# RWKV channel-major projections: inputs prepared ahead of the side work in every step, inverse of heads 0 to 7 from the 21st of 48 steps

## The chip, the cores and the metric

One core of a Trainium2 chip runs the whole forward pass as one program. The metric is the device time of one execution in microseconds; lower is better. The engines that matter here are PE (TensorE, matmuls; its weight loads are listed as PEld), DVE (VectorE), ACT (ScalarE), POOL (GpSimd) and SP, whose queue issues the loads of weights.

## The reference

A two-layer decoder trunk over 512 tokens of width 1024: layer 0 mixes tokens by RWKV-7, layer 1 by a gated MLP, and each layer also has two half-step SwiGLU networks and a cross-attention to 256 memory tokens. The change is in the RWKV-7 mixer, cut here to what matters:

```python
xr, xk, xv = (h + dx * mu[m] for m in (0, 2, 3))       # dx = token_shift(h) - h
r, k, v = xr @ Wr, xk @ Wk, xv @ Wv                    # 512x1024 @ 1024x1024 each
decay = exp(-exp(-softplus(-(w0 + tanh(xw @ w1) @ w2)) - 0.5))
a = sigmoid(a0 + (xa @ a1) @ a2)
kk = (k * k_k), each head of 64 divided by its norm
k = k * (1 + (a - 1) * k_a);  b = kk * a
for each token t, for each of 16 heads:                # state is 64x64
    sa = state @ -kk_t
    state = state * decay_t + sa b_t^T + v_t k_t^T
    y_t = state @ r_t
```

Everything is in fp32.

## The kernel before

**Numbers.** A product in fp32 is made of three matmuls on a rounded high part and a low part of both operands (`mm3`, L114 to L116). The function `split` makes the two parts: ACT casts the high part (L93) and DVE subtracts it for the low part (L98). Weights come in through `wload`: a DMA on SP's queue, then `split` into the tiles `whi` and `wlo`.

**The projection stage** is the function `rwkv_in`, in the profile from about 410 to 615 us. It makes k, r and v (in this order) with channels on the partitions for k and r. The work is cut into 48 steps: 3 projections, for each two column halves `nb`, for each 8 slices of the contraction. One step is `products(i)`: 4 tiles of 3 matmuls, 12 matmuls of 128x512 in all. The first two tiles' low-part products need `wlo` only at the third matmul, L116 for k and r.

**What a step prepares.** `prepare(i + 3)` fetches the weights of the step three ahead: one DMA of 256 KB, one ACT cast (`whi`), one DVE subtraction (`wlo`). In the first half of each projection it also mixes the token-shifted input: an ACT operation (L835), a DVE operation (L837) and a split (ACT L861, DVE L862). The pools hold three weight pairs.

**Side work.** Two kinds of generators are advanced a piece at a time by the same loop. `pump()` advances `post_k` (L994 to L1037: decay, normalisation and gates of the k half just finished) and `post_r` (L1048 to L1073: the same for r), which are mostly DVE and ACT operations on 128x512 or 64x512 tiles with a few matmuls (L975, L1028, L1029, L1072). `invert()` advances `inverse(0)` for heads 0 to 7, once `post_k(0)` is done, and after it `inverse(1)` for heads 8 to 15, once `post_k(1)` is done. The scan over chunks needs the inverses of 64x64 triangular matrices, and `inverse` builds them: scores on PE (L1156, L1163, small matmuls) with copies to `MD` (DVE L1171) and `LT` (ACT L1173), a transposition (DVE L1176), then 30 rounds of forward substitution on DVE, a multiplication and an addition each (L1186, L1193) on 31 to 256 columns, two transpositions (DVE L1203 to `A2`, L1206 to `XT`), copies, and 8 groups of small matmuls (L1225). `inverse(1)` may advance only 8 times in the loop (`ahead`); what is left of it is advanced by the scan's own `pump()` and is finished at the latest before the 9th of 16 chunks.

**Order.** Each engine executes its instructions in the order of the program. That order is made when the program is built, by a scheduler that starts from the order in which the code is written. After the 48 steps a loop finishes `inverse(0)`, and the scan begins: per chunk PE makes `sm` (L1447), DVE (L1452) and ACT copy it to `e`, PE multiplies by the inverse `TT` (L1463), DVE copies to `AV` (L1465), and so on; matmuls of the next work stand between them.

Of the kernel before, what the change touches and what calls it, by code (L numbers as in the profile page):

```python
# [20 lines left out]
KC = C // P  # L21
# [18 lines left out]
class Trunk:  # L40
# [763 lines left out]
    def rwkv_in(self, st, prologue):  # L804
# [28 lines left out]
        def xmix(m, ct):  # L833
            t1 = tp.tile([P, T], F32, tag="xm1", name="xm1")
            act(t1, hT[:, ct, 0:T], AF.Identity, scale=col(MU + m, ct))  # L835
            xm = tp.tile([P, T], F32, tag="xm2", name="xm2")
            nc.vector.scalar_tensor_tensor(  # L837
                xm, hT[:, ct, 1 : T + 1], omu[:, m, ct : ct + 1], t1, ALU.mult, ALU.add
            )
            return xm  # L840
# [10 lines left out]
        def prepare(i):  # L851
            if i >= len(steps):
                return
            p, nb, k = steps[i]
            m, wi = projs[p]
            src = ins["rwkv_w_rkv"][wi, nb, k // 2][:, (k % 2) * 512 : (k % 2) * 512 + 512]
            ws[i] = self.wload(src, 512)
            if nb == 0:
                xm = xmix(m, k)
                xh = xsp.tile([P, 2, T], F32R, tag="xs", name="xs")  # L860
                nc.scalar.copy(xh[:, 0], xm)  # L861
                nc.vector.tensor_tensor(xh[:, 1], xm, xh[:, 0].bitcast(F32), ALU.subtract)  # L862
                xs[p, k] = xh[:, 0], xh[:, 1]
# [72 lines left out]
        def lora_2(ct):  # L936

            cs = slice(ct * P, ct * P + P)
            for j, w in enumerate(w2s):
                ps = sc()  # L940
                self.mm3(ps, [z[:, cs] for z in w], tws, True, True)
                if j == 0:
                    s = tmp("sq")[:, :T]
                    act(s, ps, AF.Sigmoid, bias=col(W0, ct))
                    nc.vector.tensor_tensor_scan(L[:, ct, :], scm, s, 0.0, ALU.mult, ALU.add)
                else:
                    act(AR[ct][:, :, 64:128], c3(ps), AF.Sigmoid, bias=col(A0, ct))
# [4 lines left out]
        def pump():  # L952
            while queue:
                if next(queue[0], 1) is None:
                    break
                queue.pop(0)

        def invert():
            if inv[0] is not None:
                if ready[0] and next(inv[0], 1) is not None:  # L960
                    inv[0] = None
            elif inv[1] is not None and ready[1] and (ahead or self.ttp):
                ahead[:1] = []
                if next(inv[1], 1) is not None:
                    inv[1] = None
# [135 lines left out]
        def products(i, fs=range(4)):  # L1101
            p, nb, k = steps[i]
            x, w = xs[p, k], ws[i]
            for f in fs:
                s = slice(f * P, (f + 1) * P)
                if p == 2:
                    self.mm3(ps[f], [z[:, s] for z in x], w, k == 0, k == KC - 1)
                else:
                    self.mm3(ps[f], [z[:, s] for z in w], x, k == 0, k == KC - 1)
# [9 lines left out]
        for i in range(2, len(steps)):  # L1119
            p, nb, k = steps[i]  # L1120
            if k == 0:
                ps = [self.psum() for _ in range(4)]
            products(i)
            if i < KC:
                lora_2(i)
            else:
                pump()
                invert()
            prepare(i + 3)
            pump()  # L1130
            invert()
            if i == KC - 1:
                act(self.D, L.rearrange("p k (c t) -> p k c t", c=NCH)[:, :, :, CH - 1], AF.Exp, scale=-DECAY)
            if k == KC - 1:
                for f in range(4):
                    evacs[p](nb, f, ps[f])
# [593 lines left out]
```

## Time and profile before

| | us |
|---|---|
| median of 3 runs | 2412.9 (2410.41 to 2415.75) |
| the profiled execution, its own time | 2409.73 |
| span of the profiled execution | 2408.0 |
| PE busy | 2359.3 (98%) |
| DVE busy | 1677.4 (70%) |
| ACT busy | 1087.9 (45%) |
| POOL busy | 136.4 (6%) |

The span is what the engines' records cover; 1.7 us lie around it. Busy shares are of the whole span, in which the projection stage is one part in twelve. The granted clock is TensorE's, as a share of its full 2.4 GHz; over the whole run it was 0.995.

### The profile page before, as it was taken

To read this page: it belongs to the slowest core of one execution; us is meant where nothing else is said; L and a number is where in the kernel's file an instruction comes from. 1 tells how busy PE (TensorE), PEld (TensorE's weight loads), DVE (VectorE), ACT (ScalarE), POOL (GpSimd) and SP (SyncE) were. 2 spreads that over 40 slices of the span, in tenths; PEclk is the share of its full clock that TensorE was granted. 3 is DMA by queue.
4 is the path that set the end of the run, shared out by engine and by line. 5 is a ranking of instruction groups with operands and counts; after the bars stand their busy time and mean duration, and the time that the engine had idled before them with its cause. 6 is when DMAs were issued, how large, how long until landed. Compare 5 with 4: busy or idle time off the path is not lost.

```text
span 2408.0 us, 40219 instructions
## 1 busy us (share of the span) xinstructions
PE 2359.3 (98%) x16336; PEld 2067.2 (86%) x16336; DVE 1677.4 (70%) x2680; ACT 1087.9 (45%) x1821; POOL 136.4 (6%) x157
## 2 busy tenths in 40 slices
PE   7999999989999999999999999999999999999998
PEld 7898995757887888999998999998888888989897
DVE  7776867798877656877777787764254455969594
ACT  5443433975555344534344443443432244535252
POOL 2000001000345000000000000000000000000000
PEclk9999999999999999999999999999999999999999
DMA  4433222213444422324242323242223242233222
GB/s 144 151 100 119 88 99 71 72 46 92 121 98 110 159 88 84 117 75 133 71 132 75 113 89 119 80 153 97 88 88 96 70 132 75 84 97 122 84 97 84
DMA packets 104937, 241.65 MB, mean 100 GB/s; under 512 B 27184, under 2 KB 31280, under 8 KB 104368
## 3 DMA queue, kind: packets, MB, share of 16 engines
q1 hardware_dynamic: 98864, 225.67, 29.6%
q10 hardware_dynamic: 5888, 13.42, 1.7%
q8 instruction: 128, 2.10, 0.4%
q14 instruction: 57, 0.47, 0.1%
HBM read 227.38 MB, written 7.34 MB: 97 GB/s over the span
## 4 chain that ended last, share of the span: by engine, by line
PE 89%; DVE 5%; ACT 3%; DMA 1%; issue 1%; POOL 1%; DVEq 0%; SPq 0%; POOLq 0%; ACTq 0%
PE ps L114 27%; PE ps L116 27%; PE ps L115 27%; PE ps L217 1%; DVE wlo L98 1%; PE y L1514 1%; PE y L1515 1%; PE ps L756 1%; PE sc L1285 0%; ACT whi L93 0%; POOL wlo L96 0%; DMA m_scr<-mo 0%; PE ps L911 0%; PE sm L1479 0%; ACT BK L983 0%
## 5 line engine op out<-in xcount | busy, mean ns | idle before, releaser
L98 DVE TENSOR_TENSOR wlo<-wraw,whi 128x1024 fp32r<-128x1024 f32 (+1 forms) x264 | 281.3, 1069 | 292.5 <-ACT whi L93 277.9
L114 PE MATMUL ps<-nT_hi,whi 128*128 128x256 f32 (+1 forms) x1504 | 449.7, 301 | 4.1 <-ACT nT_hi L93 1.5
L116 PE MATMUL ps<-nT_hi,wlo 128*128 128x256 f32 (+1 forms) x1504 | 448.6, 299 | 1.2 <-POOL wlo L96 1.2
L115 PE MATMUL ps<-nT_lo,whi 128*128 128x256 f32 (+1 forms) x1504 | 449.1, 299 | 0.4 <-DVE nT_lo L98 0.3
L93 ACT CAST whi<-wraw 128x1024 fp32r<-128x1024 f32 (+1 forms) x268 | 246.0, 921 | 355.1 <-PE ps L116 227.4
L114 PEld LDWEIGHTS ps<-nT_hi,whi 128*128 128x128 f32 x1504 | 283.2, 189 | 15.6 <-ACT nT_hi L93 3.3
L115 PEld LDWEIGHTS ps<-nT_lo,whi 128*128 128x128 f32 x1504 | 284.5, 189 | 10.9 <-DVE nT_lo L98 1.5
L116 PEld LDWEIGHTS ps<-nT_hi,wlo 128*128 128x128 f32 x1504 | 284.1, 189 | 11.3 <-POOL wlo L96 1.5
L116 PE MATMUL ps<-whi,hT_lo 128*128 128x512 f32 x704 | 278.5, 396 | 0.0
L114 PE MATMUL ps<-whi,hT_hi 128*128 128x512 f32 x704 | 277.9, 395 | 0.0
L115 PE MATMUL ps<-wlo,hT_hi 128*128 128x512 f32 x704 | 277.7, 394 | 0.0
L116 PE MATMUL ps<-s_hi,wlo 128*128 128x256 f32 x960 | 271.2, 283 | 1.2 <-DVE wlo L98 1.1
L114 PE MATMUL ps<-s_hi,whi 128*128 128x256 f32 x960 | 271.0, 282 | 1.2 <-ACT whi L93 0.6
L115 PE MATMUL ps<-s_lo,whi 128*128 128x256 f32 x960 | 270.4, 282 | 0.0
L93 ACT CAST whi<-g_raw 128x1024 fp32r<-128x1024 f32 x160 | 168.1, 1050 | 200.4 <-PE ps L116 125.6
L98 DVE TENSOR_TENSOR wlo<-g_raw,whi 128x1024 fp32r<-128x1024 f32 x160 | 196.5, 1228 | 32.6 <-ACT whi L93 31.9
L116 PEld LDWEIGHTS ps<-s_hi,wlo 128*128 128x128 f32 x960 | 181.7, 189 | 2.0 <-DVE wlo L98 2.0
L114 PEld LDWEIGHTS ps<-s_hi,whi 128*128 128x128 f32 x960 | 181.6, 189 | 1.6 <-ACT whi L93 0.8
L115 PEld LDWEIGHTS ps<-s_lo,whi 128*128 128x128 f32 x960 | 181.4, 189 | 0.0
L115 PEld LDWEIGHTS ps<-wlo,hT_hi 128*128 128x128 f32 x704 | 132.6, 188 | 31.0
L116 PEld LDWEIGHTS ps<-whi,hT_lo 128*128 128x128 f32 x704 | 132.5, 188 | 30.8
L114 PEld LDWEIGHTS ps<-whi,hT_hi 128*128 128x128 f32 x704 | 132.6, 188 | 30.3
(360 smaller groups left out, 4612.2 us busy)
## 6 DMA issues: line engine op xcount, KB each, us to landing
wraw<-in_ffn_w_out_dram SPq DMA_DIRECT2D x88, 512.0 KB, 4.1
g_raw<-in_ffn_w_in_dram SPq DMA_DIRECT2D x80, 512.0 KB, 3.6
t_raw<-in_ffn_w_in_dram SPq DMA_DIRECT2D x80, 256.0 KB, 3.0
e_raw<-in_ffn_w_in_dram SPq DMA_DIRECT2D x80, 256.0 KB, 3.4
wraw<-in_rwkv_w_rkv_dram SPq DMA_DIRECT2D x48, 256.0 KB, 2.7
wraw<-in_ffn_w_in_dram SPq DMA_DIRECT2D x16, 512.0 KB, 3.6
wraw<-in_xattn_wq_dram SPq DMA_DIRECT2D x16, 512.0 KB, 3.8
wraw<-in_xattn_wo_dram SPq DMA_DIRECT2D x16, 512.0 KB, 3.6
```

What stands on the lines that cost most here:

```text
L93: r = [self.nc.scalar.copy(hi, src)]
L98: r.append(self.nc.vector.tensor_tensor(lo, src, hi.bitcast(F32), ALU.subtract))
L114: mm(ps, l[0], r[0], start=start, stop=False, **kw)
L115: mm(ps, l[0], r[1], start=False, stop=False, **kw)
L116: mm(ps, l[1], r[0], start=False, stop=stop, **kw)
L217: nc.tensor.transpose(ps[:, j * P : (j + 1) * P], xn[:, k * P : (k + 1) * P], self.ident)
L756: nc.tensor.matmul(pv[:, t * P : (t + 1) * P], v[:, t, g * P : (g + 1) * P], ws[:, g, :], start=True, stop=True,)
L1514: mm(o, rz[n % 2][:, par, i, :], SV[:, par, i, :], start=True, stop=False)
L1515: mm(o, M[:, par, i, 64:128], AV[:, par, i, :], start=False, stop=True)
```

## The change

In steps 8 to 47 `prepare(i + 3)` now stands ahead of both calls of `pump()` and `invert()`; before, one of each came first. And `invert()` is called only from step 20 on (the 21st). Steps 0 to 7 keep their order (there is nothing to invert in them). No instruction is added or removed; lines behind L1131 have numbers smaller by one after the change.

```diff
@@ -1123,12 +1123,11 @@
             products(i)
             if i < KC:
                 lora_2(i)
-            else:
+            prepare(i + 3)
+            for _ in range(2 if i >= KC else 1):
                 pump()
-                invert()
-            prepare(i + 3)
-            pump()
-            invert()
+                if i >= 20:
+                    invert()
             if i == KC - 1:
                 act(self.D, L.rearrange("p k (c t) -> p k c t", c=NCH)[:, :, :, CH - 1], AF.Exp, scale=-DECAY)
             if k == KC - 1:
```

What the scheduler makes of it is shown at three places. A row is a line of the code, an operation, and output<-inputs with their buffers' numbers; the numbers of buffers differ between the two kernels.

**DVE, ahead of the low part that came last.** Before, 43 rows stand between the low parts of the weights of step 27 and of step 28 (`wlo_5332`). The last of them are these; `X` and `tmp` are the substitution of `inverse(0)`, `sq` and `AR0` are `post_r(0)`:

```order
L1186 TENSOR_TENSOR tmp_5208<-M2_4973,X_4975 128x252
L1037 TENSOR_TENSOR AR1_3886<-AR1_3886,fe_5223 128x8x64
L1193 TENSOR_TENSOR X_4975<-X_4975,tmp_5208 128x14x18
L1050 TENSOR_TENSOR AR0_3885<-AR0_3885,em_5280 128x8x64
L1186 TENSOR_TENSOR tmp_5229<-M2_4973,X_4975 128x247
L1054 SCALAR_TENSOR_TENSOR sq_5283<-AR0_3885,cols_64,BK0_3893 64x512
L1193 TENSOR_TENSOR X_4975<-X_4975,tmp_5229 128x13x19
L1054 SCALAR_TENSOR_TENSOR sq_5283<-AR0_3885,cols_64,BK0_3893 64x512
L1186 TENSOR_TENSOR tmp_5244<-M2_4973,X_4975 128x240
L1050 TENSOR_TENSOR AR0_3885<-AR0_3885,em_5316 128x8x64
L1193 TENSOR_TENSOR X_4975<-X_4975,tmp_5244 128x12x20
L98 TENSOR_TENSOR wlo_5332<-wraw_5329,whi_5331 128x512
```

Now the low parts of steps 28 and 29 stand 7 and 10 rows behind those ahead of them, and the longest gap is the next one, 25 rows between the low parts of steps 29 and 30 (`wlo_5342`). It ends so:

```order
L1054 SCALAR_TENSOR_TENSOR sq_5286<-AR0_3885,cols_64,BK0_3893 64x512
L1185 TENSOR_TENSOR tmp_5190<-M2_5160,X_5162 128x156
L1054 SCALAR_TENSOR_TENSOR sq_5286<-AR0_3885,cols_64,BK0_3893 64x512
L1192 TENSOR_TENSOR X_5162<-X_5162,tmp_5190 128x26x6
L1050 TENSOR_TENSOR AR0_3885<-AR0_3885,em_5314 128x8x64
L1185 TENSOR_TENSOR tmp_5211<-M2_5160,X_5162 128x175
L1054 SCALAR_TENSOR_TENSOR sq_5317<-AR0_3885,cols_64,BK0_3893 64x512
L1192 TENSOR_TENSOR X_5162<-X_5162,tmp_5211 128x25x7
L1054 SCALAR_TENSOR_TENSOR sq_5317<-AR0_3885,cols_64,BK0_3893 64x512
L1185 TENSOR_TENSOR tmp_5214<-M2_5160,X_5162 128x192
L98 TENSOR_TENSOR wlo_5342<-wraw_5339,whi_5341 128x512
```

The gap is shorter by 18 rows and two steps later, and the substitution in it is at an earlier, narrower round (its last blocks have 175 and 192 elements a partition, where they had 247 and 240).

**DVE, at the start of the scan.** Before, the substitution of `inverse(1)` is over and its transpositions (L1203, L1206) stand just ahead of the first copy `e1` of the scan (L1452):

```order
L1193 TENSOR_TENSOR X_5898<-X_5898,tmp_6884 128x31
L1203 STREAM_TRANSPOSE A2_6917<-X_5898 128x32x32
L98 TENSOR_TENSOR wlo_6353<-wraw_6350,whi_6352 128x512
L1206 STREAM_TRANSPOSE XT_6954<-X_5898 128x32x32
L1452 COPY e1_6319<-sm_6314 128x128
```

Now 17 rounds of the substitution, 34 rows, are spread behind that copy, and the transpositions stand in the fifth chunk, between its `e1` and its copies to `AV`:

```order
L1451 COPY e1_6968<-sm_6963 128x128
L1185 TENSOR_TENSOR tmp_6884<-M2_6029,X_6031 128x31
L1287 TENSOR_TENSOR M_6962<-sc_6977,con_63 128x512
L1192 TENSOR_TENSOR X_6031<-X_6031,tmp_6884 128x31
L1287 TENSOR_TENSOR M_6962<-sc_6978,con_63 128x512
L1202 STREAM_TRANSPOSE A2_6917<-X_6031 128x32x32
L1205 STREAM_TRANSPOSE XT_6954<-X_6031 128x32x32
L98 TENSOR_TENSOR wlo_6999<-wraw_6996,whi_6998 128x512
L1343 TENSOR_TENSOR BK0_3893<-y_6431,g2_6952 128x4x128
L1464 COPY AV_6792<-sm_7017 64x128
L1464 COPY AV_6792<-sm_7024 64x128
```

So the first copy of the scan has lost the two transpositions ahead of it, and the fifth chunk has them.

**PE, at step 18.** Before, the first scores of `inverse(0)` follow the products of step 18:

```order
L114 MATMUL ps_4827<-xs_4706,whi_4698 128x512
L115 MATMUL ps_4827<-xs_4706,whi_4698 128x512
L975 MATMUL pn_4840<-sq_4841,con_63 128x512
L116 MATMUL ps_4827<-xs_4706,wlo_4699 128x512
L1156 MATMUL sc_4735<-AR0_3885,BK0_3893 32x64
L1163 MATMUL sc_4735<-AR0_3885,BK0_3893 32x32
```

Now the products of the next step follow at that place, and the scores stand at steps 21 (64 of them) and 26 (2 times 32) of what were 4 groups of 64:

```order
L115 MATMUL ps_4753<-xs_4694,whi_4686 128x512
L975 MATMUL pn_4779<-sq_4780,con_63 128x512
L116 MATMUL ps_4753<-xs_4694,wlo_4687 128x512
L975 MATMUL pn_4779<-sq_4791,con_63 128x512
L114 MATMUL ps_4750<-xs_4743,whi_4735 128x512
L115 MATMUL ps_4750<-xs_4743,whi_4735 128x512
L116 MATMUL ps_4750<-xs_4743,wlo_4736 128x512
```

The matmuls are the same ones, and the small ones come later.

## Rows read from the trace of the kernel before

**Rows 1.** The page: busy time by engine, and the chain that ended last.

```profile
PE 2359.3 (98%) x16336; PEld 2067.2 (86%) x16336; DVE 1677.4 (70%) x2680; ACT 1087.9 (45%) x1821; POOL 136.4 (6%) x157
...
PE 89%; DVE 5%; ACT 3%; DMA 1%; issue 1%; POOL 1%; DVEq 0%; SPq 0%; POOLq 0%; ACTq 0%
```

**Rows 2.** Busy time in stretches of the stage and of the scan.

```profile
core 0: us, PE busy (x) PEld busy (x) DVE busy (x) ACT busy (x) POOL busy (x), PEclk, DMA share, GB/s
449.00:514.00 65.00, 63.66 (x489) 45.90 (x488) 55.93 (x102) 62.98 (x108) 1.50 (x6) 1.00 0.21 67
514.00:525.00 11.00, 10.58 (x42) 6.74 (x41) 10.66 (x24) 8.92 (x15) 0.34 (x3) 1.00 0.08 25
525.00:537.00 12.00, 4.10 (x8) 1.38 (x6) 11.87 (x25) 5.77 (x10) 0.11 (x1) 0.64 0.00 1
537.00:549.00 12.00, 12.00 (x46) 8.72 (x45) 11.87 (x28) 4.41 (x8) 0.00 (x0) 0.93 0.33 109
549.00:615.20 66.20, 62.37 (x743) 47.23 (x743) 57.89 (x122) 38.35 (x74) 3.89 (x7) 1.00 0.33 94
619.30:681.20 61.90, 61.56 (x958) 54.30 (x958) 44.95 (x95) 36.90 (x86) 28.48 (x27) 0.97 0.42 100
```

**Rows 3.** PE in order of time, around its longest wait: start, us, what [idle before].

```profile
524.87 0.39 PE L114 MATMUL ps<-xs,whi 128*128 128x512 f32 x1
525.10 0.40 PE L115 MATMUL ps<-xs,whi 128*128 128x512 f32 x1
532.36 2.07 PE L975 MATMUL pb<-sq,con 128*128 128x512 f32 x2 [6.86 <-DVE sq L1054]
...
536.55 2.46 PE L116 MATMUL ps<-xs,wlo 128*128 128x512 f32 x4
```

**Rows 4.** DVE in order of time: the low parts of steps 27, 28 and 30.

```profile
513.93 0.68 DVE L98 TENSOR_TENSOR wlo<-wraw,whi 128x512 fp32r<-128x512 f32 x1
...
535.76 0.69 DVE L98 TENSOR_TENSOR wlo<-wraw,whi 128x512 fp32r<-128x512 f32 x1
...
543.49 0.69 DVE L98 TENSOR_TENSOR wlo<-wraw,whi 128x512 fp32r<-128x512 f32 x1
```

**Rows 5.** Groups of DVE, 450 to 620 us: busy us, mean ns, idle before.

```profile
L98 DVE TENSOR_TENSOR wlo<-wraw,whi 128x512 fp32r<-128x512 f32 x39 | 26.7, 684 | 2.6 <-ACT whi L93 2.4
L1193 DVE TENSOR_TENSOR X<-X,tmp 128x60 f32<-128x60 f32 (+15 forms) x60 | 20.6, 343 | 0.9
L1186 DVE TENSOR_TENSOR tmp<-M,X 128x60 f32<-128x60 f32 (+15 forms) x60 | 20.5, 342 | 1.0
L1054 DVE SCALAR_TENSOR_TENSOR sq<-AR,cols,BK 64x512 f32<-64x512 f32 x16 | 11.9, 745 | 0.3
...
L837 DVE SCALAR_TENSOR_TENSOR xm<-hT,omu,xm 128x512 f32<-128x512 f32 x14 | 10.1, 747 | 0.1
L1035 DVE SCALAR_TENSOR_TENSOR fe<-AR,nkk,sc 128x512 f32<-128x512 f32 x8 | 5.9, 744 | 1.3 <-PE sc L1029 1.1
...
L1036 DVE TENSOR_TENSOR AR<-fe,em 128x512 f32<-128x512 f32 x8 | 5.5, 688 | 0.6 <-POOL em L1032 0.5
...
L1176 DVE STREAM_TRANSPOSE M<-MD 128x1024 f32<-128x1024 f32 x2 | 4.1, 2033 | 0.0
```

**Rows 6.** Groups of ACT by form, 450 to 620 us: busy us, mean ns, idle before.

```profile
L835 ACT ACTIVATE xm<-hT,cols 128x512 f32<-128x512 f32 x12 | 8.5, 718 | 0.0
...
L1173 ACT COPY LT<-sc 32x256 f32<-32x256 f32 x16 | 5.8, 361 | 2.3 <-DVE MD L1171 2.1
```

**Rows 7.** DVE in order of time, at the first copy of the scan.

```profile
614.97 2.11 DVE L1203 STREAM_TRANSPOSE A<-X 128x1024 f32<-128x1024 f32 x1
...
617.52 1.94 DVE L1206 STREAM_TRANSPOSE XT<-X 128x1024 f32<-128x1024 f32 x1
619.30 0.28 DVE L1452 COPY e<-sm 128x128 f32<-128x128 f32 x1
```

**Rows 8.** PE in order of time, at the same place.

```profile
619.64 0.45 PE L1463 MATMUL sm<-e,TT 64*64 64x64 f32 x8 [1.68 <-DVE e L1452]
```

## The prediction

> **What bounds the kernel now.** I read the page first. PE is busy 98% of the span, and the chain that ended last is PE for 89%, DVE for 5%, ACT for 3% [rows 1]. That average hides the stage that the change touches, so I next cut it into windows [rows 2]. The reader should compare, in each, 'window length less busy time' for three engines:
>
> - 449 to 514 us (steps 9 to 26): PE 63.66 of 65.00, ACT 62.98, DVE 55.93. PE keeps its pace, ACT has no room, and DVE idles 9.1 us.
> - 514 to 549: DVE is full (10.66, 11.87 and 11.87 of 11, 12 and 12). In 525 to 537 PE has only 4.10 us of work in 12, at a granted clock of 0.64, a mix of both levels.
> - 549 to 615.2: PE 62.37 of 66.20. DVE idles 8.3 us, but PE still waits, for single results of the inverse's chain.
> - 619.3 to 681.2, the scan's first six chunks: PE 61.56 of 61.90, DVE idles 17.0 us.
>
> The hole in 525 to 537 is then read in order of time. PE's last product begins at 525.10, the next matmul of any kind at 532.36, after 6.86 us of waiting for `sq`, and the products go on at 536.55 [rows 3]. What they wait for is on DVE: the low part of step 28's weights begins at 535.76, 21.8 us after that of step 27 (513.93) [rows 4]. So the wait is one of DVE's order: the operation that PE needs is short (0.684 us, [rows 5]), but 43 others stand ahead of it. From the end of the product of 525.10 to 536.55, less the two `pb` matmuls in between, PE loses about 10 us. A smaller wait is at the scan's start: the first copy `e` begins at 619.30, straight behind the two transpositions of 2.11 and 1.94 us [rows 7], and PE waits 1.68 us for it [rows 8].
>
> **What is removed and added.** Nothing: the same instructions and DMAs, in another order. The DMAs of a step are issued by SP, which has no other work in these steps, so they can't be late through the change; at the hole the low part waits for its place on DVE, not for data. I price moves only.
>
> **1. The hole.** I add up DVE rows by their durations [rows 5]. Before, from the low part of step 27 to that of step 28: 22 substitution rows near full width, about 0.41 each, 8.9 us; 4 rows of L1035 at 0.744 and 8 of L1036 and L1037 at 0.688, 8.5; 2 of L1050 (like L1036) and 4 of L1054 at 0.745, 4.4; one each of L862, a split and L837, 2.1; and the low part itself, 0.7: 24.6 us. They took 21.8 [rows 4], because neighbours overlap a little: a factor of 0.89. Up to the low part of step 30 it was 33.3 us of durations and 29.6 by the clock (513.93 to 543.49), the same factor.
>
> After, the rows from the low part of step 27 to those of steps 28, 29 and 30 sum to 5.3, 8.3 and 13.1 us (the last: 13 narrow substitution rows 3.7, three post_k rows 2.1, three L1050 and six L1054 6.5, and the low part). That is 26.7, times 0.89 is 23.8 us. Where does it start? ACT paces the stretch before, as it is full there. Up to step 27's cast ACT loses the four `LT` copies of 0.361 and gains one L835 of 0.718 [rows 6], 0.7 us less in all, so step 27's low part begins at 513.2, not 513.93. Step 30's low part then begins at 537.0 instead of 543.5: **6.5 us earlier**.
>
> Not all of it is gain. PE had worked off about 2 us of `post_r(0)`'s sums (L975) by the end of step 30, which now come after it. So the stage is some 4.5 us ahead there: a wait of about 5.5 us at step 30 where there were about 10 at step 28. The bounds: 0, if PE's wait only moves from step 28 to 30 and is as long there; 10, if it closes.
>
> **2. What the gate at step 20 does to the early steps.** PE's 128 small-matmul pairs of `inverse(0)`'s scores leave steps 18 and 19 and stand at 21 and 26. That lets PE be earlier in between, but it is ACT that sets when weights come there, so I take 0. 18 substitution rows and the transposition L1176 (2.033) leave DVE's stretch before step 27, about 8 us of work, from where DVE idled 9.1 to where it is full. This is in sum 1 already, by the rows counted.
>
> **3. Steps 36 to 39.** In the new order the low parts of these stand 11 rows apart, 6.4 to 6.8 us of durations, about 6 by the clock, and PE does a step in 12 times 0.234 (the starts 524.87 and 525.10, [rows 3]), 2.8 us. The rows from step 30's low part to step 36's sum to 18.2 us, so that one is ready at about 537.7 + 16.2 = 554, and the next three at 560, 566 and 571.5. PE, out of step 30 at about 539.5, needs six steps and some 3 to 5 us of `pb` sums to the start of step 36: 559.5 to 561.5, then 562 to 564, 565 to 567 and 568 to 570. So it waits in step 39 and perhaps in 38, by 1.5 to 4 us; the products' first third needs no low part, and I take **+1.5**, between 0 and 4. After them there is room: all rows to step 47 sum to 145 us from step 10's low part, against 160.7 before.
>
> **4. The inverse's own waits.** The matmuls L1225 and the scores of `inverse(1)` wait for single results in 549 to 615.2, where PE idles 3.8 us [rows 2]. They move from steps 34 to 36 to steps 41 to 44, with the same dependences: 0.
>
> **5. The scan's start.** The first `e` no longer stands behind L1203 and L1206: the 1.68 us wait [rows 8] goes, **-1.6**.
>
> **6. What is given back in the scan.** 34 substitution rows at a mean of 0.343 are 11.7 us [rows 5], and the two transpositions 4.1 [rows 7]: 15.8, times 0.89 as in the hole 14 us more DVE work behind the first `e`, up to the fifth chunk. DVE has 17.0 us idle up to 681.2 [rows 2], but a good part of that idle time lies where it waits for the very matmul whose result it has to copy next, and PE is full. A row of 0.4 us ahead of such a copy costs at most itself; the pair of transpositions ahead of the fifth chunk's `AV` copies could cost what the same pair cost the first `e`, 1.68, or its whole 4.1. Bounds: 0, if all fits the idle time; 14, if none does. I take **+3**, near the row of the same pair: its 1.7 us, and 1.3 for the 34 rows.
>
> **Sum**: -4.5 + 1.5 - 1.6 + 3.0 = -1.6 us. Against its own time the profiled execution goes from 2409.7 to 2408.1; that execution was 3.2 below the median of 2412.9, so the median goes to **2411.3**. A change of under 0.2% (4.8 us) is about what a measurement of this kernel can't tell from none.
>
> The Trainium skill ("Perfetto Trace Analysis", section "Optimization Strategy") says that where the most-contended engine changes over time, a kernel may gain by interleaving the regimes. By that rule the early substitution was well placed, in a stretch with idle DVE, and the gate undoes it; alone it would bring the time up, towards rival B's 2420. The rows bear it out in part: DVE's 9.1 us idle in 449 to 514 will grow, yet the same change spreads the tail over the scan, a regime where DVE has room too.
>
> **Rivals.**
>
> A. *The scan takes the tail for nothing.* For it: 17.0 us of idle DVE against 14. Against it: the work is not spread as the idle time is, and the transpositions come in one block. Then -4.5 + 1.5 - 1.6 = -4.6; with the hole closed to nothing and no wait in steps 36 to 39, -11.6. I put it at -7: **2406**.
>
> B. *Slower: the tail costs the scan more than the loop gains.* The place is the first five chunks; the mechanism is that DVE's copies `e`, `AV` and `SV` stand behind substitution rows, and PE, which has nothing spare there (61.56 of 61.90), waits for them. At a cost of 4.6 us it eats the gain; at 9.4 us it makes the kernel slower beyond the 0.2%, and at its bound of 14 it gives +9.4. For it: each `e`, `AV` and `SV` is on the chain between chunks. Against it: with DVE busy 44.95 of 61.90 us there, PE lost only 0.3 in six chunks [rows 2]. I put it at +7: **2420**.
>
> C. *The change does not do what it says*: the wait only moves from step 28 to 30 at its old size of 10 us, since DVE, not the order, is short there, and the scan costs 1 to 2 us, what the first `e` gains: 0 to +2, **2413.5**.
>
> **How the numbers follow.** Forecast (-1.6, with its own range of -5 to +3): 0.38. A: 0.33. B: 0.18. C: 0.11. The range goes from 2403 (A with the hole nearly closed) to 2419 (B at a price of 11 in the scan) and leaves out about 2 in 10, the ends of A and of B. Faster by over 0.2%: A but for its weakest tenth, and the best tenth of the forecast, 0.34. Slower by over 0.2%: B and a little of C, 0.19. Within: 0.47.
>
> **What would show it.** In the changed kernel's trace: PE's longest wait in the stage at the L116 of step 30, about 5 us (right) or 10 (C); step 30's low part at 537 (right) or near 543; DVE's idle time in 449 to 514 up from 9 to about 16; the last product of step 47 ended near 612, not 615.2; the first `e` near 614.7 with no wait of PE ahead of L1463; and PE's waits for DVE's copies in the first six chunks 3 us in sum (right), under 1 (A), or over 9 (B). I would be wrong by the scan if its first six chunks take less than 61 or more than 71 us, and by the loop if step 47 ends outside 609 to 614.

## The result, and the profile after

The changed kernel takes 2426.4 us (median of 6 runs, 2419.5 to 2431.2) against 2411.7 for the kernel before in the same comparison (6 runs, 2406.1 to 2415.8): a ratio of 1.006, with a 95% interval of 1.0047 to 1.0073. It is slower by 14.8 us, on the side of rival B and beyond its price; the range (2403 to 2419) does not hold it. The profiled execution took 2423.2 us, its span 2421.5.

The page of the changed kernel, its span and busy time by engine, answers to [rows 1]:

```profile
span 2421.5 us, 40224 instructions
...
PE 2367.6 (98%) x16336; PEld 2071.6 (86%) x16336; DVE 1680.1 (69%) x2680; ACT 1086.0 (45%) x1821; POOL 135.9 (6%) x157
```

PE's busy time rose by 8.3 us though it executes the same 16336 matmuls. The rest of the 13.5 us is waiting. The mean granted clock of the two profiled executions is the same, 0.995, so in sum a lower clock does not explain the 8.3; single stretches differ much. I count as missing clock the length of a stretch times what its granted clock lacks of 1. Over whole executions it is 14.1 us in the mean of the changed kernel's 6 runs and 12.2 in the 15 runs of the kernel before that were timed beside e1: some 2 of the 14.8 us.

The windows of the changed kernel, with the columns of [rows 2]. The last one goes from the first copy `e` of the scan (L1452 before, L1451 now) to the seventh, as 619.30 to 681.20 did before:

```profile
core 0: us, PE busy (x) PEld busy (x) DVE busy (x) ACT busy (x) POOL busy (x), PEclk, DMA share, GB/s
449.00:514.00 65.00, 63.83 (x431) 46.15 (x430) 54.84 (x88) 64.07 (x110) 1.62 (x7) 1.00 0.22 70
514.00:525.00 11.00, 11.00 (x105) 8.03 (x104) 10.59 (x21) 9.25 (x18) 0.34 (x3) 1.00 0.15 49
525.00:537.00 12.00, 9.63 (x34) 5.74 (x33) 11.74 (x27) 4.15 (x7) 0.00 (x0) 1.00 0.07 22
537.00:549.00 12.00, 12.00 (x53) 9.29 (x52) 11.85 (x27) 6.21 (x11) 0.00 (x0) 1.00 0.34 111
549.00:573.00 24.00, 20.49 (x68) 13.26 (x68) 23.38 (x53) 9.55 (x17) 0.00 (x0) 0.93 0.21 65
573.00:615.20 42.20, 38.18 (x664) 29.34 (x663) 26.81 (x55) 25.63 (x52) 4.18 (x8) 1.00 0.37 107
614.28:694.54 80.26, 71.77 (x971) 60.92 (x967) 62.67 (x132) 38.17 (x90) 30.36 (x28) 0.89 0.34 85
```

What the reader is to see: in 525 to 537 PE is busy for 9.63 us where it had 4.10, at the full clock where it had 0.64 (with the 0.93 behind it, 5.2 us of missing clock [rows 2], which are gone). But DVE is now full from 514 to 573 (57.6 of 59.0 us) where it was full to 549, and PE idles 3.5 us in 549 to 573 and 4.0 behind it, 7.5 together against 3.8 before. And the six chunks that took 61.9 us take 80.3: PE idles 8.5 us there where it idled 0.3, and is busy 10.2 us longer for nearly the same matmuls at a mean clock of 0.89 where it was 0.97.

Where the time went, from the two traces. The changed kernel's profiled execution ends the third step 2.3 us earlier (its next matmul starts at 422.81, before at 425.08), ahead of anything that differs, so I add 2.3 to its times:

| place | before | after, +2.3 | difference |
|---|---|---|---|
| products of step 30 end | 546.4 | 537.1 | -9.3 |
| products of step 47 end | 615.2 | 614.9 | -0.3 |
| first copy `e` of the scan | 619.3 | 616.6 | -2.7 |
| seventh copy `e` | 681.2 | 696.8 | +15.7 |
| sixteenth copy `e` | 772.7 | 787.9 | +15.2 |

So there are two results to explain: the loop wins 9.3 us at the hole and gives all of it back by step 47, and the scan pays 18.4 us for what was put into it, between the first copy and the seventh.

**The hole.** PE in order of time in the changed kernel:

```profile
529.73 1.12 PE L975 MATMUL pb<-sq,con 128*128 128x512 f32 x2 [0.59 <-DVE sq L1054]
532.63 1.12 PE L975 MATMUL pb<-sq,con 128*128 128x512 f32 x2 [1.77 <-DVE sq L1054]
533.62 1.20 PE L116 MATMUL ps<-xs,wlo 128*128 128x512 f32 x4
```

The wait has moved to step 30, as forecast, but it is down to 2.4 us in two pieces, both for `sq` ahead of the `pb` sums; against [rows 3] the 2.07 us of a pair of `pb` matmuls at the low clock are 1.12 here.

**The scan.** DVE in the first chunk of the changed kernel:

```profile
614.28 0.28 DVE L1451 COPY e<-sm 128x128 f32<-128x128 f32 x1
...
614.93 1.15 DVE L1192 TENSOR_TENSOR X<-X,tmp 128x255 f32<-128x255 f32 x1
...
618.64 1.26 DVE L98 TENSOR_TENSOR wlo<-wraw,whi 128x512 fp32r<-128x512 f32 x1
619.82 0.47 DVE L1464 COPY AV<-sm 64x128 f32<-64x128 f32 x2
620.22 1.36 DVE L98 TENSOR_TENSOR wlo<-wraw,whi 128x512 fp32r<-128x512 f32 x1
```

and POOL at the same time:

```profile
614.64 1.17 POOL L1294 TENSOR_TENSOR BK<-BK,D 128x512 f32<-128x512 f32 x1 [11.16 <-PE sc L1284]
618.31 1.04 POOL L1310 TENSOR_TENSOR v<-v,bon 128x512 f32<-128x512 f32 x1 [2.50 <-DMA AV<-v]
619.43 1.60 POOL L1313 TENSOR_TENSOR v<-v,ln 128x512 f32<-128x512 f32 x1
```

The addition on 255 columns takes 1.15 us instead of 0.42, the subtraction of 0.68 takes 1.26 and 1.36, and each ends 0.3 to 0.6 us behind the end of a POOL operation that began ahead of it (615.8, 619.4, 621.0). The two copies out of PSUM at 619.82 run beside POOL's at their usual pace. Counted over 610 to 690 us, DVE operations that lasted over 0.25 us more than the shortest of their form lasted 7.8 us too long in all; in the kernel before it was 3.6 (612 to 675). The Trainium skill ("SBUF — State Buffer", section "SBUF: two separate sides") says this much: a DVE operation with two inputs in SBUF and a GpSimd operation that reads SBUF exclude each other for the whole instruction. The rows agree, in the direction in which POOL came first.

PE's two largest waits in the scan, in order of time:

```profile
628.60 0.50 PE L1317 MATMUL sc<-g,sg 128*128 128x512 f32 x1 [1.97 <-DVE M L1287]
...
652.75 0.74 PE L1462 MATMUL sm<-e,TT 64*64 64x64 f32 x14 [1.91 <-DVE e L1451]
```

The rows of DVE and of POOL ahead of the second of them:

```profile
648.25 1.21 DVE L1185 TENSOR_TENSOR tmp<-M,X 128x207 f32<-128x207 f32 x1
649.39 1.76 DVE L1357 TENSOR_TENSOR v<-v,BK 128x512 f32<-128x512 f32 x1
651.07 1.21 DVE L1192 TENSOR_TENSOR X<-X,tmp 128x207 f32<-128x207 f32 x1
652.32 0.29 DVE L1451 COPY e<-sm 128x128 f32<-128x128 f32 x1
```

```profile
647.86 1.37 POOL L1310 TENSOR_TENSOR v<-v,bon 128x512 f32<-128x512 f32 x1
649.31 1.29 POOL L1313 TENSOR_TENSOR v<-v,ln 128x512 f32<-128x512 f32 x1
650.56 1.49 POOL L1294 TENSOR_TENSOR BK<-BK,D 128x512 f32<-128x512 f32 x1
```

At their shortest in this trace these three DVE operations ahead of `e` take 0.37, 0.67 and 0.36 us, so they are 2.8 us too long together, more than the 1.91 us that PE waits for `e`. The windows around the two waits:

```profile
625.00:629.00 4.00, 2.03 (x20) 1.59 (x17) 3.87 (x8) 0.41 (x1) 1.27 (x1) 1.00 0.65 130
629.00:633.00 4.00, 4.00 (x30) 2.96 (x30) 2.63 (x7) 1.52 (x4) 0.00 (x0) 0.53 0.03 8
633.00:637.00 4.00, 4.00 (x43) 3.66 (x40) 2.04 (x5) 0.02 (x1) 1.57 (x2) 0.61 0.00 0
637.00:641.00 4.00, 4.00 (x56) 3.61 (x55) 2.35 (x6) 2.45 (x6) 0.19 (x1) 1.00 0.34 52
...
649.00:653.00 4.00, 2.09 (x30) 1.78 (x30) 3.97 (x6) 0.26 (x2) 2.98 (x3) 1.00 0.60 142
653.00:657.00 4.00, 3.10 (x20) 1.95 (x17) 2.94 (x9) 1.07 (x3) 0.00 (x0) 0.52 0.22 70
657.00:661.00 4.00, 4.00 (x27) 3.32 (x27) 3.08 (x10) 0.88 (x2) 0.00 (x0) 0.50 0.00 0
661.00:665.00 4.00, 4.00 (x41) 3.71 (x40) 2.71 (x7) 0.81 (x2) 3.33 (x4) 0.70 0.01 2
```

After each of the two waits the granted clock falls to the lower of its two levels (1.2 in place of 2.4 GHz): means of 0.53 and 0.61 in 8 us, then 0.52, 0.50 and 0.70 in 12 us. The missing clock there, 0.47 and 0.39 of 4 us and 0.48, 0.50 and 0.30 of 4 us, is 8.6 us, more than the two waits themselves. Of the 18.4 us in the scan 8.2 are PE idle and 10.2 are PE busy for longer; 6.7 of these are the clock (8.6 less the 0.03 of 61.9 us that were missing before), and 3.5 remain, in part 13 more matmuls that fall into the stretch.

### The profile page after: what moved, and what is told of

It is laid out like the page before. It is cut to its first block, busy times and chain, and to the rows that moved or that the text cites. A ratio compares the mean times of both kernels' runs of the same rounds, so it can differ in the third digit from the quotient of the medians.

```text
span 2421.5 us, 40224 instructions
## 1 busy us (share of the span) xinstructions
PE 2367.6 (98%) x16336; PEld 2071.6 (86%) x16336; DVE 1680.1 (69%) x2680; ACT 1086.0 (45%) x1821; POOL 135.9 (6%) x157
## 4 chain that ended last, share of the span: by engine, by line
PE 85%; DVE 6%; ACT 5%; issue 1%; DMA 1%; POOL 1%; SPq 0%; DVEq 0%; POOLq 0%; ACTq 0%
PE ps L116 26%; PE ps L114 26%; PE ps L115 26%; DVE wlo L98 1%; ACT whi L93 1%; PE ps L217 1%; PE ps L756 1%; ACT BK L983 1%; PE y L1513 1%; PE y L1514 1%; DVE tmp L1185 0%; DVE X L1192 0%; POOL wlo L96 0%; DVE sq L1054 0%; PE sc L1284 0%
```

## The experiments

Each was timed in 5 or more runs against the kernel before on the same chip. Theory "tail": the loss is the tail of inverse(1), put into the scan by the gate. Rival "order": it comes of preparing first.

**The two halves of the change apart, e1_gate and e2_first.** The gate alone:

```diff
             else:
                 pump()
-                invert()
+                if i >= 20:
+                    invert()
             prepare(i + 3)
             pump()
-            invert()
+            if i >= 20:
+                invert()
```

> Only the gate: invert() from step 20 on, prepare(i + 3) stays between the two calls as before. Theory 'tail': the loss is made by the gate, which puts 17 rounds of substitution of inverse(1) and its two transpositions behind the first copy of the scan; then this kernel is slower than before by 11 to 19 us (the change: 14.8), and its scan up to the sixth first copy (L1452) is longer than before's by 15 to 20 us. Rival 'order': the loss is made by preparing first, which spreads the low parts of steps 36 to 39; then this kernel is within 4 us of before.

The order alone:

```diff
-            else:
-                pump()
-                invert()
             prepare(i + 3)
-            pump()
-            invert()
+            for _ in range(2 if i >= KC else 1):
+                pump()
+                invert()
```

> Only the order: prepare(i + 3) ahead of both calls, invert() as early as before. Theory 'tail': the transpositions stand ahead of the first copy of the scan as before, the longest gap between two low parts on DVE is 34 rows where it was 43, so faster than before by 2 to 6 us, with a scan as long as before's. Rival 'order': slower than before by 8 to 16 us.

Measured: the gate alone 2423.4 against 2410.5, a ratio of 1.0048 (1.0035 to 1.0060), 12.9 us slower. The order alone 2412.1 against 2410.5, 1.0009 (0.9999 to 1.0018): no difference. So the loss is the gate's, and the order is free; but the gain that "tail" forecast for the order (2 to 6 us) did not come. The runs of the order alone have 16.2 us of missing clock in the mean, against 12.2 in the kernel before beside them, so 4 us of clock may hide a gain.

**More of the tail, e5_ahead0, and the same tail over fewer chunks, e3_ahead20.** Both change one number of `ahead = list(range(8))`: to 0 in the kernel before, to 20 in the changed one.

> The kernel before, but inverse(1) gets no advance at all in the 48 steps (a list of no items for its eight), so that all of its 30 rounds and its transpositions stand in the scan, where they end ahead of the ninth chunk. Theory 'tail': slower than before by 12 to 30 us, the loss between the first copy of the scan and the eighth. Rival 'order' (work of this kind costs the scan little): within 4 us of before, or faster by the 1.7 us of the first copy's wait.

> The changed kernel, but inverse(1) may advance 20 times in the loop in place of 8; the scheduler then ends its substitution in the third chunk of the scan where it was the fifth, with the same rows behind the first copy. Theory 'tail': the amount decides, so slower than before by 11 to 19 us, as the change. A rival to that: its length over chunks decides, since each row waits in front of copies; then 4 to 8 us better than the change.

Measured: e5 2423.7 against 2410.5, 1.0045 (1.0031 to 1.0059), 13.2 slower; e3 2423.5, 1.0051 (1.0038 to 1.0064), 13.0 slower. In e5 the loop is 7 us shorter (step 47 ends at 607.4 where it was 615.2, with a third step that ends 0.6 earlier), and the scan pays more than that back. Not only DVE rows have moved there: the 256 score matmuls of inverse(1) are in e5's scan too. e3's shorter tail costs as much as the long one, as "tail" forecast, but in another way. Its third chunk alone takes 29.7 us, where it took 9.0 before, in part because matmuls of later chunks, which then run shorter, stand in it:

```profile
642.20:671.90 29.70, 27.25 (x402) 23.81 (x399) 17.54 (x33) 17.51 (x37) 7.17 (x6) 0.77 0.39 107
```

There 6.8 us of clock are missing. PE waits 0.9 us for a low part and 1.2 us for a copy of ACT (L587) that stands behind ACT's four copies to `TT` of the inverse (651.7 to 655.9 us), and the low level follows. In 655 to 658 us DVE and POOL are both idle. DVE's lengthened rows sum to 5.5 us in e3's scan, against 7.8 in the changed kernel and 3.6 before. So the equal times do not show that the amount alone decides.

The scan from the first copy `e` to the seventh in e1_gate, e2_first and e5_ahead0, in this order, with the columns of the windows above:

```profile
617.56:696.33 78.77, 70.17 (x970) 60.03 (x968) 62.51 (x130) 37.35 (x88) 30.61 (x28) 0.91 0.35 86
```

```profile
618.94:680.75 61.81, 61.48 (x958) 54.25 (x958) 44.92 (x94) 36.80 (x86) 27.85 (x27) 0.97 0.43 99
```

```profile
608.49:688.70 80.21, 73.29 (x1034) 63.30 (x1029) 69.78 (x156) 33.39 (x82) 29.87 (x28) 0.96 0.33 81
```

The kernels with the tail in the scan take 78.8 and 80.2 us for it, the one without takes 61.8, as before. (e5 has still more of the tail behind the seventh copy: up to the ninth it takes 105.9 us where the kernel before takes 82.5.)

**POOL relieved in the scan, e6_after_less_pool and e7_before_less_pool.** The same edit in the changed kernel and in the kernel before:

```diff
             b = self.BKq[q][:, :, c, :]
+            if q == 0:
+                for k in range(4):
+                    nc.scalar.activation(b[:, k], b[:, k], AF.Identity, scale=D[:, k, c : c + 1])
+                return
             nc.gpsimd.tensor_tensor(b, b, D[:, cof(q), c : c + 1].to_broadcast([P, 4, P]), ALU.mult)
...
+            if q:
+                nc.gpsimd.tensor_tensor(
+                    v3, v3, self.bon[:, t, 8 * q : 8 * q + 8].unsqueeze(2).to_broadcast([P, 8, 64]), ALU.mult
+                )
+                nc.gpsimd.tensor_tensor(v, v, ln[:, 1], ALU.add)
```

> The changed kernel with POOL relieved in the scan's first eight chunks: the decay of b (L1294) is done by four ACT operations in its place, and the two operations on v ahead of the gate (L1310, L1313: the bonus and the norm's bias of heads 0 to 7) are left out, so the output of these heads lacks them. DVE's instructions stand as in the changed kernel. Theory 'held up by POOL': part of the loss is DVE operations with two inputs that last 0.4 to 1.1 us longer while POOL works (7.8 us of such lengthening between 610 and 690 us, 3.6 before), and PE's clock that falls after the waits so caused; then the distance to the equally relieved kernel of before (the next run) shrinks from 14.8 to 6 to 11 us. Rival 'rows alone': the distance stays at 13 to 17.

> The kernel before with the same relief of POOL, the reference for the run ahead; it leaves out the same bonus and bias. Both theories: within 4 us of before, since PE waits less than 0.4 us in the scan's first six chunks.

Measured: e6 2416.4 against 2410.2, 1.0023 (1.0013 to 1.0032); e7 2410.1 against 2410.2, 0.9994 (0.9984 to 1.0003). The distance between the two is 6.3 us where it was 14.8, as the theory forecast (6 to 11). The scan from the first copy to the seventh, in e6 and then in e7:

```profile
619.85:687.49 67.64, 64.39 (x973) 55.51 (x969) 56.00 (x132) 45.61 (x114) 14.86 (x16) 1.00 0.39 101
```

```profile
617.36:679.51 62.15, 61.23 (x958) 54.03 (x958) 43.20 (x94) 43.87 (x110) 14.56 (x16) 0.97 0.42 100
```

DVE's rows stand as in the changed kernel, but for two that come a few places later, and the scan costs 5.5 us more than its reference instead of 18.4; the clock is 1.00 throughout. The same two operations in e6 that lasted 1.15 and 1.26 us:

```profile
620.50 0.42 DVE L1192 TENSOR_TENSOR X<-X,tmp 128x255 f32<-128x255 f32 x1
...
623.48 0.68 DVE L98 TENSOR_TENSOR wlo<-wraw,whi 128x512 fp32r<-128x512 f32 x1
```

So 12.9 of the 18.4 us in the scan go when POOL is relieved. By the windows 5.8 of them are PE's waits (8.2 more than before, 2.3 more than in e7) and 8.6 the clock (6.7 more missing than before, 1.9 less than in e7); the rest goes the other way by 1.5. In e6 the three rows ahead of the fourth `e` take 0.36 to 0.68 us and PE's wait of 1.91 is gone, so there the lengthened rows did make PE wait. That the clock falls because of such waits is only supported: in e3 it falls without POOL at work, in e6 it does not fall after a wait of 1.9 us. Also, ACT does the decay in POOL's place, so POOL is not the only engine whose work differs. Over whole executions the clock weighs less: 11.5 us are missing in the mean of e6's runs and 12.8 in e7's, so some 3 of the 8.5 us by which the distance shrank are the clock. e6's loop is some 4 us longer than the changed kernel's (618.3 at step 47, with a third step that ends 1.6 later); most of that is the clock, which is 0.92 in 573 to 618.3 us, 3.6 us missing, where the changed kernel has 1.00 behind 573.

**DVE's rows handed to POOL in the loop, e8_pool_low and e9_pool_low5.** The low parts of the weights of steps 27 to 36 (e9: 27 to 31) are made by POOL:

```diff
-            ws[i] = self.wload(src, 512)
+            ws[i] = self.wload(src, 512, nc.gpsimd if 27 <= i < 37 else None)
```

> The kernel before, but the low parts of the weights of steps 27 to 36 are made by POOL, so that they no longer stand behind 43 rows of DVE. Theory 'DVE's sum': the time is set by all that DVE has to do from 514 us to the transposition A2 at 554 us; ten rows less (6 us) bring that transposition and what follows forward, less what POOL's own operations hold DVE up: -1 to -5 us. Rival 'the hole alone': the wait for the low part goes with all of its 10 us: -7 to -11 us. Rival 'held up by POOL' in full: ten operations of 1.1 us each hold DVE up for as long as they take: 0 to +5 us.

> As the run ahead, with the low parts of steps 27 to 31 alone on POOL. Theory 'DVE's sum': half as much, 0 to -3 us. Rival 'the hole alone': as much as the run ahead, -7 to -11 us, since the longest gap is step 28's. Rival 'held up by POOL' in full: 0 to +3 us.

Measured: e8 2421.4 against 2410.2, 1.0045 (1.0031 to 1.0058), 11.2 slower; e9 2415.9, 1.0023 (1.0013 to 1.0032), 5.8 slower. Both are slower than any theory had it. PE's wait for the low part of step 28 is gone, and `A2`, the transposition that ends the substitution of heads 0 to 7, comes later instead, at 562.0 in e8 and 556.4 in e9 where it was 554.1. POOL and DVE in e8, one pair of rows of each:

```profile
551.68 1.41 POOL L96 TENSOR_TENSOR wlo<-wraw,whi 128x512 fp32r<-128x512 f32 x1 [3.33 <-ACT whi L93]
```

```profile
551.86 1.78 DVE L1054 SCALAR_TENSOR_TENSOR sq<-AR,cols,BK 64x512 f32<-64x512 f32 x1
...
562.03 2.16 DVE L1203 STREAM_TRANSPOSE A<-X 128x1024 f32<-128x1024 f32 x1
```

An operation of 0.745 us takes 1.78 behind POOL's. Ten subtractions of 0.684 less for DVE, and its chain ends 8 us later. "The hole alone" falls with these two, and that POOL holds DVE up is borne out again. But the times do not measure it: 21.8 us of clock are missing in the mean of e8's runs and 17.9 in e9's, against 12.9 in the kernel before beside them, so 8.9 of the 11.2 us and 5.0 of the 5.8 can be the clock. In e8's trace it is at 0.64 in 573 to 591 us, behind the late `A2`.

**The hole shortened by holding other work back, e10_hold30, e11_first_hold34, e12_three.** e10 (e11 the same until step 34, with the preparation first):

```diff
             else:
-                pump()
+                if i < 24 or i >= 30 or not ready[1]:
+                    pump()
                 invert()
             prepare(i + 3)
-            pump()
+            if i < 24 or i >= 30 or not ready[1]:
+                pump()
             invert()
```

> The kernel before, but post_r(0) is held back until step 30: from step 24 pump() is not called once post_k(1) is done. The longest gap between low parts on DVE falls from 43 to 31 rows, and the next ones follow by 1 to 5 rows. Theory 'DVE's sum': the rows ahead of the transposition A2 are as many as before (it is row 668 in both), so its end stays at 556 us within 2 us and with it the kernel's time, within 3 us of before, though PE's long wait at step 28 shortens by 5 us or more. Rival 'the hole alone': faster by 4 to 9 us.

> As the run ahead with post_r(0) held until step 34 and prepare(i + 3) ahead of both calls: the longest gap is 28 rows. In the scan the transposition XT of inverse(1) stands behind the first copies. Theory 'DVE's sum': within 4 us of before. Rival 'the hole alone': faster by 6 to 11 us.

e12 adds to the kernel before:

```diff
             pump()
             invert()
+            if 18 <= i < 30:
+                invert()
```

> The kernel before with a third invert() in steps 18 to 29: the substitution of heads 0 to 7 is offered earlier. On DVE the order moves little: A2 stands at row 668 as before. All theories: within 3 us of before.

Measured against 2409.2: e10 2410.4, 1.0006 (0.9997 to 1.0014); e11 2415.1, 1.0021 (1.0013 to 1.0030); e12 2409.4, 1.0005 (0.9996 to 1.0014). In e10 PE's longest wait falls from 6.86 to 4.76 us and `A2` stays, at 551.2 in a trace whose third step ends 2.4 us earlier, so 553.6 against 554.1:

```profile
527.83 2.07 PE L116 MATMUL ps<-xs,wlo 128*128 128x512 f32 x4 [4.76 <-DVE wlo L98]
```

```profile
551.15 2.15 DVE L1205 STREAM_TRANSPOSE A<-X 128x1024 f32<-128x1024 f32 x1
```

"DVE's sum" holds for e10 and e12; e11 is 5.9 us slower, outside both forecasts. Its loop ends 5 us earlier (608.0 where it was 615.2, with a third step that ends 2.0 earlier), and it loses more than that in the first three chunks (34.0 us where they took 28.0); both transpositions of inverse(1) stand in the second (624.1 and 635.4 us).

**DVE relieved for good, e13_copies_act and e14_hold30_act.** Six copies go to ACT; e14 adds the hold of e10.

```diff
-            nc.vector.tensor_copy(bs, pb)
+            nc.scalar.copy(bs, pb)
...
-            nc.vector.tensor_copy(MD[:, hs, :], ps[:, :, 0:32])
+            (nc.scalar.copy if q else nc.vector.tensor_copy)(MD[:, hs, :], ps[:, :, 0:32])
```

> The kernel before with six copies taken from DVE to ACT: the two copies of post_r's sums (L1068, 0.68 us each) and the four MD copies of inverse(1) (L1171, 0.42 each), 3.0 us of DVE. The longest gap of 43 rows stays. Theory 'DVE's sum': what DVE has to do from 514 us to the first copy of the scan sets the time, so 1 to 3 us faster than before with the hole at step 28 as long as before. Rival 'the hole alone': within 1 us of before.

> The same six copies on ACT together with post_r(0) held until step 30, which alone shortened the long wait and gave nothing in time. Theory 'DVE's sum': 2 to 5 us faster than before, as the relief lets the loop's 3 us stand, XT staying one row behind the first copy of the scan. Rival 'the hole alone': as the hold alone, within 2 us of before.

Measured against 2410.0: e13 2407.4, 0.9995 (0.9986 to 1.0004); e14 2410.0, 1.0003 (0.9993 to 1.0014). e13's time is not to be told from before's; in its trace the ninth copy `e` comes 2.2 us earlier than before (697.3, which is 699.6 with 2.3 added, against 701.8), within the 1 to 3 us of the forecast. e14's forecast failed: the loop ends 2.4 us earlier, and PE waits 3.85 us at the scan's start for the first `e`, one more time behind a transposition of inverse(1). No version here beats the kernel before beyond doubt.

## Why the prediction was wrong

**The step that failed is number 6, what is given back in the scan.** I took 3 us, with 14 as the bound; it measured 18.4: 8.2 of PE's waits, 6.7 of clock and 3.5 of matmuls recorded longer or more of them. Two things were left out. The first is POOL: I counted DVE rows at the durations that they had in the loop, where POOL does next to nothing (1.5 us of 65, [rows 2]); in the scan it works 28.5 of 61.9, and that number stood in the same row. A substitution row has two inputs in SBUF and waits for POOL there, and with POOL relieved the 8.2 us of waits became 2.3. The second is the clock, which my sum put at nothing. PE's waits alone stay under my bound of 14; with the clock the cost is beyond it. The place and the kind of the loss, DVE's copies behind the moved rows, were named in step 6 and in rival B; rival B's price (up to +9.4) had the same two gaps.

The clock was left out on both sides. In the traces the shorter hole gives back 5.2 us of it, steps 36 to 39 cost 1.7 and the scan 6.7. Over whole executions that comes to some 2 us, so most of the 14.8 is not the clock.

**Step 1, the hole: right in kind, too small.** Step 30's low part starts at 532.9, or 535.2 on before's scale; forecast 537.0. From the low part of step 27 it took 24.1 us, forecast 23.8; what was off is the start, 2.1 us earlier than I had it. The "about 10 us" that PE loses at the old hole was misread: two pairs of `pb` matmuls stand in it, not one, and PE idles 7.9 us of 525 to 537 [rows 2]. That became 2.4, a gain of 5.5 where I had 4.5. The stage was 9.3 us ahead at step 30: these 5.5, and the 5.2 that the clock gives back there, less some 1.4 of other work of PE.

**Step 3, steps 36 to 39: wait of 1.5 forecast, 3.5 found** in 549 to 573, within the bound of 4. The low parts stand 6.0, 5.9 and 5.6 us apart, as worked out (6). But PE does not wait for them, so the size is right by luck:

```profile
557.30 0.56 PE L114 MATMUL ps<-whi,xs 128*128 128x512 f32 x1 [1.55 <-ACT xs L861]
...
568.74 0.50 PE L114 MATMUL ps<-whi,xs 128*128 128x512 f32 x1 [1.39 <-ACT xs L861]
```

These two and one of 0.31 us are for the mixed input, which ACT casts (L861) once DVE has made it (`xm`, L837): the same full DVE, another row. The granted clock of 0.93 there takes another 1.7.

**Step 4, the inverse's own waits: forecast 0.** They moved to steps 41 to 44 as said, but behind 573 PE idles 4.0 us, together with 549 to 573 7.5 where it idled 3.8. So of the 9.0 us that the loop gives back, 3.7 are idle time, 1.7 the clock and about 2 the `pb` sums that I had named; 1.6 remain unexplained. The likely reason behind it is what e2, e10 and e14 point to: a shorter hole brought no time in any of them (in e2 the clock may have hidden a gain). DVE is full until the substitution of heads 0 to 7 is over, PE needs its result (`A2`) for work that stands in its queue, and `A2` ended within 0.6 us of the old time in e2, e10 and e12. Moving rows ahead of it or behind it moves PE's wait. That DVE's sum is the bound is only supported: taking 3 us of it away brought 2.2 in e13's trace and no difference that its times can tell.

**Step 2** was right that the early steps gain nothing (step 26 ends at 519.2 on before's scale, before 519.1). DVE's idle time in 449 to 514 did not grow to 16, only to 10.2, since other rows moved into it. **Step 5** was right: no wait ahead of L1462, and the first `e` gains 2.4 us on the loop; forecast 1.6.

**Interleaving regimes.** The rule that the prediction cites from the Trainium skill ("Perfetto Trace Analysis", section "Optimization Strategy") spoke against the gate. e1 bears it out in sign. But the loss was not where the rule would look, at DVE's room in 449 to 514; it was in the regime into which the work was put.

## What to carry to other kernels

Before work is moved into another stage, read there what every engine does, those included that do not seem to bind: a price from the old stage holds only where the neighbours are the same. For a DVE operation with two SBUF inputs look at POOL's busy time first. Set the granted clock beside every idle time that you price, where it shrinks as well as where it grows, and compare it over whole executions before you call a difference its doing. And when a wait is removed, ask which result the waiting engine needs next after it; if that one's time does not move, neither does the end.

## What the runs showed of the hardware

DVE operations of 0.42 to 0.75 us on SBUF inputs lasted 1.15 to 1.78 us when a POOL operation had begun ahead of them, while copies out of PSUM beside POOL kept their pace. Handing ten subtractions (6.8 us of DVE) to POOL made DVE's chain 8 us longer. After waits of 1.9 to 2 us of PE in the scan 3.4 and 5.1 us of clock were missing, so it was at the lower level for some 7 and 10 us; in e6, whose largest waits there were 1.9 and 1.0 us, it stayed at 1.00, so a wait of that size does not always cost the clock.
